# Sums of squares in three parts, two accumulators and two-slot rows in a two-layer hybrid kernel

## The chip, the cores and the metric

The kernel runs on one core of a Trainium2 chip. The metric is the device time of one execution in microseconds. PE is the matrix engine (TensorE), DVE is VectorE, ACT is ScalarE, POOL is GpSimd, and SP is the engine whose queue issues the DMAs.

## The reference

Two layers work on 640 tokens: 128 context tokens and 512 latent ones, of width 1024. The even layer's mixer is an mLSTM (4 heads) beside an HGRN2 (4 heads); the odd layer's is differential attention (8 heads). Each layer also has an FFN, and adaLN vectors (shift, scale, gate) that are computed from a conditioning vector. Cut to what the change touches:

```python
def _rmsnorm(x, g):
    xf = x.astype(f32)
    return xf * lax.rsqrt(jnp.mean(xf * xf, axis=-1, keepdims=True) + EPS) * g.astype(f32)

def _modulation(cond, w, b):
    mod = jnp.einsum('...d,de->...e', jax.nn.silu(cond.astype(f32)), w.astype(f32)) + b.astype(f32)
    return jnp.split(mod[..., None, :], 6, axis=-1)

# mLSTM, a chunk: the decay between two tokens weights the scores
dmat = jnp.where(tri, b[..., :, None] - b[..., None, :] + ic[..., None, :], -jnp.inf)
s = jnp.einsum('bhtd,bhsd->bhts', qc, kc) * jnp.exp(dmat - mt[..., None])

# a layer
hp = _rmsnorm(xp, norm_mix_g[l]) * (1.0 + sc_p) + sh_p    # and hs from xs alike, then the mixer
xp = xp + g_p * mp
hp = _rmsnorm(xp, norm_ffn_g[l]) * (1.0 + sc2_p) + sh2_p  # then the FFN
```

After the two layers a last RMSNorm gives the outputs.

## The kernel before

**Layout and order.** The residual `x` lies with features on partitions, as [128, 8, 640]: 8 blocks of 128 features, and the tokens as two halves of 320. A float32 product is three matmuls of high and low parts (`mm3`, whose matmuls all carry line 188). A scheduler orders each engine's instructions; in the mixer units and in the transitions PE keeps the order in which the program is written. The mixers run as eight units, four mLSTM heads and four HGRN2 heads. Between the steps of a unit, a `fill` object feeds PE with projection matmuls of coming units; it also holds a list of side jobs, which take their turn once so much matmul cost has been issued.

**The adaLN side units.** Most adaLN vectors are products on PE, but four units of four column blocks each run on ACT and GpSimd beside the mLSTM heads (`ada_vec`, L477 to L502). A unit loads 8 blocks of 256 KB of the weight (`araw`, two slots in the space of the tag `fb`, L483), multiplies each by the two conditioning vectors on ACT (16 products, L486, into `acc` or `atmp`), and adds them on GpSimd (14 adds of 128x512, L488). Then PE sums over partitions with four matmuls (`pj<-acc,ones`, L492), the result is copied, transposed and finished. There is one accumulator, in the space of the tag `qp`, and one unit is open at a time (the fourth argument of `add_side`, L1248). Ahead of the first HGRN2 unit (`u == H4`, L1249) all side jobs still open are carried out, and the HGRN2 work then takes over the tags `qp`, `fb`, `kc` and `kr`.

**The rows of the decay.** For each mLSTM head and each chunk of 128 tokens two rows of the decay are spread over all partitions by a DMA of 128 KB from DRAM on SP's queue (`rows_of`, L915). The tile `nb` has five slots in the space of the tag `kr`; the rows of head h + 1 are fetched chunk by chunk as VectorE's min with the causal mask (`weights`, L960) frees a slot, so the fetch is five chunks ahead. After the min come two exponentials on ACT (L964) and VectorE's product with the scores (L965).

**The norms.** `sq_sum` (L523) squares the 8 blocks of one half on ACT (L530). Blocks 1 to 5 are added to `sq` by GpSimd for half 0 and by VectorE for half 1 (L532); block 7 is added to block 6 in `s2` by VectorE (L534), which then joins the two (L535). `columns` (L592) takes the mean over the 1024 features for 64 tokens a matmul (5 for a half), adds epsilon on VectorE (`r`, L598), takes the power -1/2 on GpSimd (L599) and makes a diagonal on VectorE (`dg`, L601), which one more matmul spreads over the partitions (`spread`). Both run in three transitions: from the first mixer to its FFN, from there to the second layer's mixer, and from that to its FFN. The output norm (`to_output`, `chunk`) uses `sq_sum` too.

**The lambda vector.** The second transition also loads the four lambda rows of the odd layer (`lp`) and reduces them on VectorE (L1593 to L1598).

## Time and profile before

| | us |
|---|---|
| median of 3 runs | 1824.48 (1822.47 to 1824.6) |
| the profiled execution | 1827.93 |
| its span | 1826.1 |
| PE busy | 1739.6 (95%) |
| VectorE busy | 1379.0 (76%) |
| ScalarE busy | 805.2 (44%) |
| GpSimd busy | 493.5 (27%) |

The mean clock granted to PE is 0.983 of full speed. The span goes from the first to the last recorded instruction; the execution's own time is 1.8 us more. A line like `261.62 1.07 PE L188 MATMUL pj<-acc,ones ... [9.40 <-POOL acc L488]` says that PE's matmul into the bank `pj` starts at 261.62 us and takes 1.07 us, and that PE was idle for 9.40 us before it, until GpSimd's instruction of line 488 on `acc` ended.

### The profile page before, as it was taken

The page shows a single profiled execution, that of the slowest core. Times are in us where ns is not written, and L with a number is a line of the kernel's source. Part 1 is how long each engine was busy: PE and PEld are TensorE (multiplying, and loading weights), DVE is VectorE, ACT ScalarE, POOL GpSimd, SP SyncE. Part 2 cuts the span into 40 slices and gives each one's busy share as a digit, 9 for nine tenths or more (in the row PEclk, how much of TensorE's full clock was granted, in tenths as well). Part 3 has the DMA queues.
Part 4 walks back from the last instruction along what each step waited for, and adds up shares of the span by engine and source line. Part 5 has one row for each costly group of instructions (what it writes and reads, how often), then busy time and mean ns, then how long its engine had stood idle before and what let it go on. Part 6 is the DMA issues. An engine that isn't in the chain of part 4 may idle for free.

```text
span 1826.1 us, 31627 instructions
## 1 busy us (share of the span) xinstructions
PE 1739.6 (95%) x12198; PEld 1661.5 (91%) x12198; DVE 1379.0 (76%) x2806; ACT 805.2 (44%) x1677; POOL 493.5 (27%) x409
## 2 busy tenths in 40 slices
PE   7998979999889999999999899999989999999998
PEld 5798969999778999999998898999978999999998
DVE  5657766677797777777778687777879887888787
ACT  5466543343353333333324466566536332333334
POOL 2244443233122222223211221112121333232321
PEclk9999989999989999999999999999999999999999
DMA  9344222122615434443412221112031322222211
GB/s 310 116 133 133 82 79 58 53 75 66 208 50 162 125 120 137 137 141 116 128 58 81 67 86 44 31 54 76 24 121 58 93 79 84 82 81 76 87 59 59
DMA packets 187979, 174.80 MB, mean 96 GB/s; under 512 B 7762, under 2 KB 168372, under 8 KB 187828
## 3 DMA queue, kind: packets, MB, share of 16 engines
q1 hardware_dynamic: 186564, 172.63, 30.7%
q8 instruction: 97, 1.59, 0.4%
q14 instruction: 54, 0.44, 0.1%
q10 hardware_dynamic: 1264, 0.14, 0.1%
HBM read 167.99 MB, written 4.74 MB: 95 GB/s over the span
## 4 chain that ended last, share of the span: by engine, by line
PE 76%; DVE 12%; DMA 4%; ACT 4%; issue 3%; POOL 1%; SPq 1%; ACTq 0%; DVEq 0%; POOLq 0%
PE pj L188 59%; PE nm L188 8%; PE p L188 5%; PE s L188 2%; DMA araw<-in_ada_w_dram 2%; DVE wl L319 2%; PE p L193 1%; DVE x L371 1%; ACT wh L318 1%; ACT atmp L486 1%; DVE hl L570 1%; DMA raw<-in_ffn_w_dram 1%; DMA wg<-in_ev_w_in_dram 0%; DVE hh L564 0%; PE pj L193 0%
## 5 line engine op out<-in xcount | busy, mean ns | idle before, releaser
L188 PE MATMUL pj<-hh,wh 128*128 128x320 f32 x1648 | 526.6, 322 | 11.9 <-DVE hh L564 5.7
L188 PE MATMUL pj<-hh,wl 128*128 128x320 f32 x1648 | 513.7, 312 | 0.0
L188 PE MATMUL pj<-hl,wh 128*128 128x320 f32 x1648 | 502.6, 313 | 2.1 <-DVE hl L570 1.9
L188 PEld LDWEIGHTS pj<-hh,wh 128*128 128x128 f32 x1648 | 313.1, 190 | 27.0 <-DVE hh L564 9.4
L188 PEld LDWEIGHTS pj<-hl,wh 128*128 128x128 f32 x1648 | 310.5, 190 | 3.9 <-DVE hl L570 2.4
L188 PEld LDWEIGHTS pj<-hh,wl 128*128 128x128 f32 x1648 | 313.8, 190 | 0.0
L188 PE MATMUL pj<-t,wh 128*128 128x320 f32 x960 | 217.0, 311 | 0.2 <-ACT wh L1322 0.2
L318 ACT CAST wh<-raw 128x1024 fp32r<-128x1024 f32 x127 | 132.6, 1048 | 184.8 <-PE pj L188 88.1
L319 DVE TENSOR_TENSOR wl<-raw,wh 128x1024 fp32r<-128x1024 f32 x127 | 162.8, 1284 | 40.0 <-ACT wh L318 39.7
L188 PEld LDWEIGHTS pj<-t,wh 128*128 128x128 f32 x960 | 160.9, 188 | 3.4 <-DVE o L1374 0.8
L1322 ACT CAST wh<-s 128x1024 fp32r<-128x1024 f32 x80 | 84.1, 1051 | 151.7 <-PE pj L188 151.7
L188 PE MATMUL pj<-t,wl 128*128 128x320 f32 x480 | 148.9, 310 | 1.1 <-DVE wl L1323 1.1
L1336 POOL TENSOR_TENSOR s<-raw 128x512 f32<-128x512 f32 x40 | 55.9, 1397 | 333.1 <-DVE wl L1323 331.5
L371 DVE SCALAR_TENSOR_TENSOR x<-nm,g2h,x 128x128 f32<-128x128 f32 (+1 forms) x236 | 93.5, 429 | 48.7 <-PE nm L188 48.3
L188 PE MATMUL pj<-ah,wh 128*128 128x320 f32 x392 | 122.5, 313 | 0.0
L188 PE MATMUL pj<-al,wh 128*128 128x320 f32 x392 | 121.3, 310 | 0.0
L188 PE MATMUL pj<-ah,wl 128*128 128x320 f32 x392 | 121.2, 309 | 0.0
L371 DVE SCALAR_TENSOR_TENSOR x<-pj,g2h,x 128x128 f32<-128x128 f32 (+2 forms) x292 | 112.1, 430 | 12.0 <-PE pj L188 11.3
L1338 POOL TENSOR_TENSOR s<-s,raw 128x512 f32<-128x512 f32 x40 | 66.4, 1659 | 198.3 <-DVE wl L1323 198.3
L1323 DVE TENSOR_TENSOR wl<-s,wh 128x1024 fp32r<-128x1024 f32 x80 | 97.2, 1215 | 8.5 <-ACT wh L1322 8.4
L1322 ACT CAST wh<-raw 128x512 fp32r<-128x512 f32 (+1 forms) x81 | 67.9, 838 | 80.1 <-PE pj L188 80.0
L188 PE MATMUL nm<-al,wh 128*128 128x320 f32 x312 | 96.3, 311 | 1.6 <-DVE al L1438 1.6
(415 smaller groups left out, 3898.4 us busy)
## 6 DMA issues: line engine op xcount, KB each, us to landing
raw<-in_ffn_w_dram SPq DMA_DIRECT2D x132, 512.0 KB
own<-in_ada_w_dram SPq DMA_DIRECT2D x48, 512.0 KB
raw<-in_ev_w_in_dram SPq DMA_DIRECT2D x36, 512.0 KB
raw<-in_od_w_in_dram SPq DMA_DIRECT2D x24, 512.0 KB
raw<-in_ada_w_dram SPq DMA_DIRECT2D x20, 512.0 KB
araw<-in_ada_w_dram SPq DMA_DIRECT2D x32, 256.0 KB
araw<-in_ada_w_dram SPq DMA_DIRECT2D x12, 512.0 KB
raw<-in_ev_w_out_dram SPq DMA_DIRECT2D x8, 512.0 KB
```

The lines of the kernel that those rows point to most:

```text
L188: ins = nc.tensor.matmul(*args, **kw)
L193: ins = nc.tensor.transpose(*args, **kw)
L318: S.copy(wh, raw3)
L319: V.tensor_tensor(wl, raw3, wh.bitcast(F32), op=ALU.subtract)
L371: V.scalar_tensor_tensor(x[:, m, t0:t1], o[:, t0 - a * HALF:t1 - a * HALF], gate[:, m, c:c + 1], x[:, m, t0:t1], op0=ALU.mult, op1=ALU.add)
L486: S.activation(t, r, AF.Copy, scale=cpad[:, k, c:c + 1])
L570: order(V.tensor_tensor(hl[:, k, t], tmps[k], hh[:, k, t].bitcast(F32), op=ALU.subtract))
L1322: S.copy(wh, src)
L1323: V.tensor_tensor(wl, src, wh.bitcast(F32), op=ALU.subtract)
L1336: G.tensor_tensor(sa[:, 0], a21, a22, op=ALU.add)
L1338: G.tensor_tensor(sb[:, 0], sa[:, 0], a11, op=ALU.subtract)
```

## The change

Three parts, each of a few lines.

- **Two accumulators.** Two side units may be open at a time, and their accumulators alternate between the spaces of `kr` and `qp`. `araw` and `atmp` keep two slots each.
- **Rows in two slots.** The rows of the decay lie in two slots of the tile `sc`, in the order of all 20 (head, chunk) pairs, and each min fetches the rows two ahead. There are 20 fetches as before, 2 at the start and 18 within the heads.
- **Norms.** GpSimd adds the squares of blocks 1 to 5 in both halves. The squares of blocks 6 and 7 are not added: `sq_sum` returns the three partial sums, and each column of `columns` and `chunk` is three matmuls that accumulate in PSUM. 36 adds of 128x320 leave VectorE, 20 of them come to GpSimd, and PE has 72 more matmuls: in a transition 15 for a half in place of 5, in the output norm 18 in place of 6.

```diff
             if 0 < k < SQUARES:
-                (V if a else G).tensor_tensor(sq, sq, dst, op=ALU.add)
-            elif k > SQUARES:
-                V.tensor_tensor(s2, s2, dst, op=ALU.add)
-        V.tensor_tensor(sq, sq, s2, op=ALU.add)
-        return sq
+                G.tensor_tensor(sq, sq, dst, op=ALU.add)
+        return sq, s2, dst
...
             for i in range(NC64):
-                T.matmul(o[0:64, i:i + 1], lhsT=sq[:, i * 64:(i + 1) * 64], rhs=mean1, start=True, stop=True)
+                for j, part in enumerate(sq):
+                    T.matmul(o[0:64, i:i + 1], lhsT=part[:, i * 64:(i + 1) * 64], rhs=mean1, start=j == 0, stop=j == 2)
...
-    nb = ev.tile([P, NCH, 2, P], F32, tag="kr", name="nb", bufs=1)
-
-    def rows_of(h, c):
-
-        Q.dma_start(nb[:, c], nmd[h, c:c + 1].to_broadcast([P, 2, P]))
+    nb = tt("sc", 1)[:, 0:4 * P].rearrange("p (i r t) -> p i r t", i=2, r=2)
+
+    def rows_of(i):
+
+        h, c = divmod(i, NCH)
+        Q.dma_start(nb[:, i % 2], nmd[h, c:c + 1].to_broadcast([P, 2, P]))
...
-            V.tensor_tensor(dm, nb[:, c], caus, op=ALU.min)
-            if h + 1 < H4:
-                rows_of(h + 1, c)
+            i = h * NCH + c
+            V.tensor_tensor(dm, nb[:, i % 2], caus, op=ALU.min)
+            if i + 2 < H4 * NCH:
+                rows_of(i + 2)
...
+            accs = [0]
+
             def acc():
-                return ev.tile([P, 2, NT], F32, tag="qp", name="acc", bufs=1)[:, :, 0:512]
+                accs[0] += 1
+                a = ev.tile([P, 2, NT], F32, tag=("qp", "kr")[accs[0] % 2], name="acc", bufs=1)
+                return a[:, :, 0:512]
...
-            fill.add_side([ada_vec_gen(*i, raw, tmp, acc) for i in vec_units(VEC0)], VEC_EVERY, 1, eager=False)
+            fill.add_side([ada_vec_gen(*i, raw, tmp, acc) for i in vec_units(VEC0)], VEC_EVERY, 2, eager=False)
```

What stands where after the change, at three places. In the rows, xN counts equal instructions in a row, and the lines of the changed kernel are its own (L916 is the fetch of rows, L925 and L926 the state loads of a head, L946 the store of a state).

First, the queue of SP at the beginning of mLSTM head 3, whose state loads are the two into `cs`; `araw` are the loads of the side units, `raw` those of weights, `nb` or `sc` the rows of the decay. Before:

```order
L483 DMA araw<-in_ada_w_dram 128x512
L926 DMA cs<-in_state_mlstm_C_dram 128x128
L927 DMA cs<-in_state_mlstm_C_dram 128x128
L947 DMA out_mlstm_C_dram<-cf 128x2x128
L325 DMA raw<-in_ev_w_in_dram 128x8x128
L483 DMA araw<-in_ada_w_dram 128x512 x3
L325 DMA raw<-in_ev_w_in_dram 128x8x128
L483 DMA araw<-in_ada_w_dram 128x512 x2
L325 DMA raw<-in_ev_w_in_dram 128x8x128
L483 DMA araw<-in_ada_w_dram 128x512
L1138 DMA hst<-in_state_hgrn_S_dram 128x128
L483 DMA araw<-in_ada_w_dram 128x512
```

After:

```order
L483 DMA araw<-in_ada_w_dram 128x512
L916 DMA sc<-nmd 128x256
L483 DMA araw<-in_ada_w_dram 128x512 x3
L1061 DMA raw<-in_ev_w_in_dram 128x4x256
L916 DMA sc<-nmd 128x256
L483 DMA araw<-in_ada_w_dram 128x512
L916 DMA sc<-nmd 128x256
L925 DMA cs<-in_state_mlstm_C_dram 128x128
L926 DMA cs<-in_state_mlstm_C_dram 128x128
L916 DMA sc<-nmd 128x256
L946 DMA out_mlstm_C_dram<-cf 128x2x128
L325 DMA raw<-in_ev_w_in_dram 128x8x128
```

The seven loads of the fourth unit, which stood behind the state loads and the store `out_mlstm_C`, are no longer there; the last `araw` now stands ahead of the state loads, and fetches of rows stand where there were none.

At the same place of the program, GpSimd from the state copies of head 0 (the first two `cs`) on; `rst` is the power for a head's norm factors. Before:

```order
L928 COPY cs<-v_746 128x1
L929 COPY cs<-v_746 128x1
L488 TENSOR_TENSOR acc<-acc,atmp 128x512 x11
L948 COPY nout<-cf 128x2
L488 TENSOR_TENSOR acc<-acc,atmp 128x512 x3
L928 COPY cs<-v_746 128x1
L929 COPY cs<-v_746 128x1
L948 COPY nout<-cf 128x2
L689 TENSOR_TENSOR rst<-rst,mhalf 128x5
L488 TENSOR_TENSOR acc<-acc,atmp 128x512 x14
L928 COPY cs<-v_746 128x1
L929 COPY cs<-v_746 128x1
```

After:

```order
L927 COPY cs<-v_746 128x1
L928 COPY cs<-v_746 128x1
L488 TENSOR_TENSOR acc<-acc,atmp 128x512 x12
L947 COPY nout<-cf 128x2
L488 TENSOR_TENSOR acc<-acc,atmp 128x512 x13
L927 COPY cs<-v_746 128x1
L928 COPY cs<-v_746 128x1
L488 TENSOR_TENSOR acc<-acc,atmp 128x512 x2
L947 COPY nout<-cf 128x2
L488 TENSOR_TENSOR acc<-acc,atmp 128x512 x2
L687 TENSOR_TENSOR rst<-rst,mhalf 128x5
L488 TENSOR_TENSOR acc<-acc,atmp 128x512 x13
```

Before, the adds of one unit lie ahead of head 0's `rst`; now those of two units and one add of the third do.

Second, VectorE in the second transition, second half of the tokens; `r` and `dg` are the norm's factors and their diagonal, `l`, `ls` and `nl` belong to the lambda vector, `p` is a PSUM bank. Before:

```order
L570 TENSOR_TENSOR hl<-hf,hh 128x320
L534 TENSOR_TENSOR s_10876<-s_10876,s_10894 128x320
L570 TENSOR_TENSOR hl<-hf,hh 128x320
L535 TENSOR_TENSOR sq<-sq,s_10876 128x320
L598 TENSOR_SCALAR r<-p_10964 64x5
L1593 TENSOR_TENSOR l_11144<-lp 1x128
L1595 TENSOR_REDUCE ls<-l_11144 1x2
L601 TENSOR_TENSOR dg<-ident,r 64x320
L1598 SCALAR_TENSOR_TENSOR nl<-ls 1x1
```

After:

```order
L567 TENSOR_TENSOR hl<-hf,hh 128x320
L319 TENSOR_TENSOR wl<-raw,wh 128x1024
L567 TENSOR_TENSOR hl<-hf,hh 128x320
L1597 TENSOR_TENSOR l_11176<-lp 1x128
L1599 TENSOR_REDUCE ls<-l_11176 1x2
L1602 SCALAR_TENSOR_TENSOR nl<-ls 1x1
L596 TENSOR_SCALAR r<-p_10986 64x5
L599 TENSOR_TENSOR dg<-ident,r 64x320
```

The two joining adds of `sq` are gone, and the three ops of the lambda vector, which stood around the diagonal, are all ahead of `r`.

Third, GpSimd in the first transition, from the last add of the first half on; `r` is the power of the first half's factors, `s<-raw` are adds on weights of the FFN. Before:

```order
L532 TENSOR_TENSOR sq<-sq,s_5490 128x320
L1337 TENSOR_TENSOR s<-raw 128x512
L599 TENSOR_TENSOR r<-r,mhalf 64x5
L1336 TENSOR_TENSOR s<-raw 128x512
L1338 TENSOR_TENSOR s<-s,raw 128x512
L1339 TENSOR_TENSOR s<-raw,s 128x512
```

After:

```order
L532 TENSOR_TENSOR sq<-sq,s_5490 128x320
L532 TENSOR_TENSOR sq<-sq,s_5665 128x320
L1341 TENSOR_TENSOR s<-raw 128x512
L532 TENSOR_TENSOR sq<-sq,s_5668 128x320
L597 TENSOR_TENSOR r<-r,mhalf 64x5
L1340 TENSOR_TENSOR s<-raw 128x512
L532 TENSOR_TENSOR sq<-sq,s_5671 128x320
L1342 TENSOR_TENSOR s<-s,raw 128x512
L532 TENSOR_TENSOR sq<-sq,s_5674 128x320
L1343 TENSOR_TENSOR s<-raw,s 128x512
L532 TENSOR_TENSOR sq<-sq,s_5677 128x320
```

The five adds of the second half, which VectorE had, lie among these; two of them stand ahead of the power.

## Rows read from the trace of the kernel before

**Rows 1.** The page, parts 1 and 4: busy time of each engine (share of the span, instructions), and the chain that ended last by line.

```profile
PE 1739.6 (95%) x12198; PEld 1661.5 (91%) x12198; DVE 1379.0 (76%) x2806; ACT 805.2 (44%) x1677; POOL 493.5 (27%) x409
...
PE pj L188 59%; PE nm L188 8%; PE p L188 5%; PE s L188 2%; DMA araw<-in_ada_w_dram 2%; DVE wl L319 2%; PE p L193 1%; DVE x L371 1%; ACT wh L318 1%; ACT atmp L486 1%; DVE hl L570 1%; DMA raw<-in_ffn_w_dram 1%; DMA wg<-in_ev_w_in_dram 0%; DVE hh L564 0%; PE pj L193 0%
```

**Rows 2.** Busy time of each engine in five windows of 5 us at the end of mLSTM head 3: window, length, then busy us (instructions) of each engine, the clock granted to PE as a share of full speed, the DMA share and GB/s.

```profile
245.00:250.00 5.00, 2.36 (x17) 1.98 (x16) 3.94 (x7) 2.47 (x8) 2.48 (x2) 0.98 0.60 172
250.00:255.00 5.00, 2.22 (x9) 1.82 (x7) 3.13 (x9) 4.23 (x11) 2.50 (x2) 0.50 0.23 66
255.00:260.00 5.00, 0.00 (x0) 0.00 (x0) 3.17 (x6) 2.01 (x5) 3.87 (x4) 0.50 0.52 157
260.00:265.00 5.00, 3.23 (x13) 1.53 (x14) 3.29 (x3) 1.57 (x4) 4.18 (x4) 0.50 0.00 0
265.00:270.00 5.00, 5.00 (x37) 5.00 (x36) 2.18 (x4) 0.00 (x0) 1.17 (x1) 0.81 0.01 3
```

**Rows 3.** PE's timeline at the same place: start, us, instruction, and in brackets the idle time before it and what ended that.

```profile
249.17 0.27 PE L193 MATMUL p<-ident,nout 128*8 128x128 f32 x1 [2.64 <-issue]
...
251.75 0.47 PE L188 MATMUL pj<-hh,wl 128*128 128x320 f32 x1
261.62 1.07 PE L188 MATMUL pj<-acc,ones 128*32 128x256 f32 x4 [9.40 <-POOL acc L488]
```

**Rows 4.** The chain of waits followed back from 310 us: start, us, what. One row of mLSTM head 1 (the load of a row of the decay) and four of the fourth adaLN unit.

```profile
157.61 2.18 DMA nb<-nmd
...
222.80 4.12 DMA araw<-in_ada_w_dram
...
251.55 2.63 DMA araw<-in_ada_w_dram
254.26 1.34 ACT atmp L486 x2
255.62 3.29 DMA araw<-in_ada_w_dram
```

**Rows 5.** GpSimd's timeline, columns as in rows 3: where the adds of the second adaLN unit and of the fourth begin, and a later pair of the fourth.

```profile
134.66 5.55 POOL L488 TENSOR_TENSOR acc<-acc,atmp 128x512 f32<-128x512 f32 x4
...
231.96 2.54 POOL L488 TENSOR_TENSOR acc<-acc,atmp 128x512 f32<-128x512 f32 x2 [16.22 <-ACT atmp L486]
...
245.49 2.48 POOL L488 TENSOR_TENSOR acc<-acc,atmp 128x512 f32<-128x512 f32 x2 [1.18 <-ACT atmp L486]
```

**Rows 6.** VectorE's timeline at the end of head 3.

```profile
245.50 1.34 DVE L987 TENSOR_SCALAR hs<-inter,dn 128x128 f32<-128x128 f32 x1
...
250.23 0.29 DVE L987 TENSOR_SCALAR hs<-inter,dn 128x128 f32<-128x128 f32 x1
...
254.56 0.48 DVE L1049 SCALAR_TENSOR_TENSOR so<-so,pj 128x320 f32<-128x320 f32 x1
```

**Rows 7.** Windows as in rows 2: unit 0 runs in the first, none in the second, unit 1 in the third, unit 2 in the fourth.

```profile
88.00:112.00 24.00, 23.23 (x157) 22.65 (x156) 10.47 (x15) 17.01 (x30) 19.90 (x15) 1.00 0.56 166
112.00:134.00 22.00, 21.25 (x146) 19.75 (x146) 14.34 (x47) 13.84 (x45) 0.98 (x4) 1.00 0.41 121
134.00:166.00 32.00, 26.17 (x181) 25.12 (x180) 28.23 (x52) 21.62 (x49) 20.87 (x17) 1.00 0.47 141
185.00:208.00 23.00, 22.47 (x154) 21.91 (x153) 19.58 (x44) 15.08 (x35) 18.46 (x14) 1.00 0.38 115
```

**Rows 8.** VectorE's timeline in head 1: the mins that use rows of the decay.

```profile
120.95 0.43 DVE L960 TENSOR_TENSOR dm<-nb,caus 128x256 f32<-128x256 f32 x1
...
127.34 0.42 DVE L960 TENSOR_TENSOR dm<-nb,caus 128x256 f32<-128x256 f32 x1 [0.24 <-PE p L188]
```

**Rows 9.** Waits of SP's queue between 60 and 270 us: line, waited for, us in total, times, the longest.

```profile
SPq L483 <- ACT atmp L486: 17.0, 11, 4.2
```

**Rows 10.** The sums of squares by their tile: operation and count, then ns (least, median, most), first and last start; the last two rows tell who waited for them (us, times).

```profile
L532 POOL TENSOR_TENSOR sq<-sq,s x20: 867/877/882, 491.4 to 1806.1; 128x320 f32<-128x320 f32 x20
L532 DVE TENSOR_TENSOR sq<-sq,s x20: 473/480/2623, 500.6 to 1812.5; 128x320 f32<-128x320 f32 x20
...
L188 PE MATMUL pj<-mean,sq x10: 189/197/198, 500.4 to 500.9; 128*64 128x1 f32 x10
...
L535 DVE TENSOR_TENSOR sq<-sq,s x8: 472/481/1452, 499.7 to 1816.5; 128x320 f32<-128x320 f32 x8
...
  PE p L188: 2.7, 1
  PE pj L188: 1.4, 1
```

**Rows 11.** PE's timeline in the first transition: the column sums of one half.

```profile
500.35 0.71 PE L188 MATMUL pj<-mean,sq 128*64 128x1 f32 x10 [1.42 <-DVE sq L535]
```

**Rows 12.** VectorE's timeline in the second transition (second half of the tokens) and in the third.

```profile
1011.41 0.28 DVE L1593 TENSOR_TENSOR l<-lp 1x128 f32<-1x128 f32 x1 [4.23 <-DMA lp<-in_od_lambda_dram]
...
1011.93 0.47 DVE L601 TENSOR_TENSOR dg<-ident,r 64x320 f32<-64x320 f32 x1
...
1361.32 2.62 DVE L532 TENSOR_TENSOR sq<-sq,s 128x320 f32<-128x320 f32 x1 [0.32 <-ACT s L530]
```

**Rows 13.** GpSimd's timeline in the third transition.

```profile
1361.18 1.17 POOL L599 TENSOR_TENSOR r<-r,mhalf 64x5 f32<-64x5 f32 x1
```

**Rows 14.** The diagonal of the norm's factors by its tile: who waited for it (us, times).

```profile
  PE p L188: 3.5, 2
```

More of the change, by code (lines that the diff above doesn't have):

```diff
@@ L1012, in ml_mix @@
         mix["last"] = last
-    for c in range(NCH):
-        rows_of(0, c)
+    for i in range(2):
+        rows_of(i)
     def hg_bounds():
@@ L1847, in chunk @@
                     if t0 < t1:
-                        T.matmul(o[t0 - c * P:t1 - c * P, 0:1], lhsT=sqs[a][:, t0 - a * HALF:t1 - a * HALF],
-                                 rhs=mean1, start=True, stop=True)
+                        for j, part in enumerate(sqs[a]):
+                            T.matmul(o[t0 - c * P:t1 - c * P, 0:1], lhsT=part[:, t0 - a * HALF:t1 - a * HALF],
+                                     rhs=mean1, start=j == 0, stop=j == 2)
                 V.tensor_scalar(rcol[:, c:c + 1], o[:, 0:1], EPS, None, op0=ALU.add)
```

## The prediction

> **What bounds the kernel now.** I read the page first, then the busy time in short stretches, then the timelines of PE, GpSimd and VectorE where PE is idle. PE is busy for 95% of the span and its projection matmuls alone are 59% of the chain that ended last [rows 1]. So time comes back only where PE stands idle or runs at a low clock, and every matmul added beside busy PE work costs its full time.
>
> The one large hole is at 245 to 270 us, at the end of the last mLSTM head. In five windows of 5 us PE is busy 2.36, 2.22, 0.00, 3.23 and 5.00 us [rows 2], an idle sum of 2.64 + 2.78 + 5.00 + 1.77 = 12.2 us. Behind the idle the granted clock reads 0.50 (the level of 1.2 GHz) in three windows and 0.81, between the two levels, in the last, against 0.98 ahead of it. Work at 0.50 takes twice its time, so 2.22 x 0.5 + 3.23 x 0.5 + 5.00 x 0.19 = 3.7 us more are lost. The hole costs 15.9 us.
>
> What ends it is the fourth adaLN unit: PE's `pj<-acc,ones` waits 9.40 us for GpSimd's add at L488 [rows 3]. The chain of waits says why it is late [rows 4]: its first load is issued at 222.80, and then load (2.63 to 4.12 us) and two ScalarE products (1.34 us) follow each other in series, up to the last load at 255.62. The load couldn't start earlier: all units share one accumulator (`qp`), which the third unit's matmul on PE gives back only then, though GpSimd is idle ahead of 231.96 for 16.22 us [rows 5].
>
> **Part 1: two accumulators.** By the order of SP's queue, the fourth unit's loads, which stood behind the state loads of head 3 (L926, L927), now stand ahead of them; on GpSimd no add stands behind head 3's copies. The stretches thus shift by one unit: unit 1, which ran from 134.66 on [rows 5], runs directly behind unit 0, unit 2 in the stretch of unit 1, unit 3 in that of unit 2.
> The gain: the 15.9 us of the hole. The 2.64 us ahead of 249.17 are counted as gone too, since VectorE ops there run slow beside the adds: L987 takes 1.34 us at 245.50, beside GpSimd's adds at 245.49, and 0.29 us at 250.23 [rows 5, 6].
> What is late next: the projection behind the hole needs a bank that VectorE empties (`so`, L1049) at 254.56 + 0.48 = 255.04 [rows 6], 2.8 us after PE fell idle at 252.2. With the slow ops in front of it gone it comes earlier; bounds 0 and 2.8, I take 1.0, nearer to the lower end because a good 2 us of slow ops precede it.
> The cost: unit 1 now runs at about 112 to 135 us, where none ran. With a unit running, PE loses 24 - 23.23 = 0.8, 32 - 26.17 = 5.8 and 23 - 22.47 = 0.5 us in the three stretches; in 112 to 134, without one, 0.75 [rows 7]. The mean of the three is 2.4; head 0's power of the norm factors now stands on GpSimd behind all of unit 1's adds, and I add 1.1, less than one 1.27 us add. Taken 3.5, bounds 0 and 7 (the worst stretch and one add).
> Sum: -15.9 + 1.0 + 3.5 = -11.4, bounds -15.9 and -6.1.
>
> **Part 2: rows in two slots.** The first accumulator's partner takes the space of the rows' five slots, so rows are loaded two ahead. A row's slot comes free with V's min (L960), and the next but one min wants it: the shortest such spacing is 120.95 to 127.34, 6.4 us [rows 8]. The load needs 2.18 us [rows 4] and about 0.4 us of issue, so alone it is in time. Ahead of it on SP's queue may stand an adaLN load that waits for ScalarE: 11 such waits, 17.0 us, the longest 4.2 [rows 9]. 2.18 + 0.4 + 4.2 = 6.8 passes the shortest spacing by 0.4. Behind a late row wait the exponentials and the head's products. Taken +0.5, bounds 0 and 3.
>
> **Part 3: the norms.** Off VectorE go 20 adds of the second half and 16 joining adds, each 0.48 us, 17 us in all; onto GpSimd come 20 adds of 0.88 us, 17.5 us [rows 10]. Neither engine bounds the span. On the path stand these:
> PE's column sums, 3 matmuls in place of 1. The first call took 0.71 us for 10 records of about 0.197 us [rows 10, 11], so a step of (0.71 - 0.197) / 9 = 0.057 us; 20 more records are 1.14 us, six calls 6.8 us. In the output norm the extra ones stand in a tail with idle PE, and I add 0.5: +7.3.
> Where PE waits for the sum (2.7 and 1.4 us, [rows 10]), two adds of 0.48 leave the chain: -0.95 in three transitions and once in the output, -3.8.
> In the third transition VectorE's add took 2.62 us beside GpSimd's power at 1361.18 [rows 12, 13]. That add leaves VectorE, and the factors' diagonal behind it gets ahead by 2.62 - 0.48 = 2.1. It is what PE waits for, 3.5 us in two places [rows 14]: -2.1.
> In the first transition two more adds of 0.88 us stand ahead of the power on GpSimd, of which none or both may fall into idle time: between 0 and 1.8, taken +0.9.
> In the second, VectorE's order puts the first op on the lambda vector (`l<-lp`, L1593) ahead of the factors `r` and the diagonal, and it waited for its load until 1011.41 [rows 12]. Before, only the diagonal (1011.93) stood behind it, while the power of 1.17 us ran beside the wait. Now `r`, the power and the diagonal come after the load: about +2.2, less up to 1 because the load's own wait starts earlier: +1.7.
> Sum: 7.3 - 3.8 - 2.1 + 0.9 + 1.7 = +4.0. VectorE's 17 us of relief gives something back where its work ends a wait of PE, which the rows don't price singly; I take -1 for it and so +3.0. Bounds: if all waits of these rows vanish (-2.7 - 1.4 - 3.5) and half the calls' matmuls hide in them (+3.4), -4.2; if nothing comes back, 7.3 + 1.8 + 2.2 = +11.3.
>
> **A rule that speaks against it.** The row at 245.50 shows a VectorE op held for 1.05 us beside GpSimd adds of 1.24 each [rows 5, 6], and 1361.32 one held for 2.1 us [rows 12]. The Trainium skill, "SBUF — State Buffer", section "SBUF: two separate sides", calls the port pair that the two engines share an exclusive lock: of a GpSimd op and a VectorE op in a two-port mode or with two SBUF inputs, the one that starts first has the pair for its whole instruction, and the other stands still. The trace agrees (0.29 against 1.34 us). By it in full, the 34 adds that change their place would hold up VectorE for their 35.3 us, and the sum would be +23.9; by the rows of the stretches with a unit it is the 3.5 above.
>
> **The rivals.**
> 1. More comes back. Unit 1 is covered like the first and third (0.8 in place of 3.5), nothing is late behind the hole (0 in place of 1.0), the norms end at -3: -15.9 + 0.8 + 0.5 - 3.0 = -17.6, a median of 1806.9. For it: PE lost only 0.8 and 0.5 us in two stretches of three. Against: PE pays for each added matmul beside busy work.
> 2. The gain is mostly eaten. Unit 1 costs 5.8 as at 134 to 166, the emptied bank is late by 2.8, the norms cost +6: -15.9 + 5.8 + 2.8 + 0.5 + 6.0 = -0.8, 1823.7. For it: 134 to 166 is the same kind of stretch (head 0 ends, head 1 begins).
> 3. Slower, through GpSimd and VectorE holding each other up. 14 adds of unit 1 (1.27 us each, 17.8) and 20 of the norms (17.5) now lie in stretches where VectorE feeds PE, 35.3 us in all. If a VectorE op on PE's path stands still for half of each, that is 17.7 us in place of unit 1's 3.5: -15.9 + 1.0 + 17.7 + 0.5 + 3.0 = +6.3, 1830.8. It decides from a third of each add on (11.4 / 35.3 = 0.32). Against: the stretches at 88 and 185 us hold as many adds (19.90 and 18.46 us of GpSimd) and PE lost 0.8 and 0.5 us [rows 7].
> 4. The second accumulator does nothing, because the raw rows have two slots only: 0 + 0.5 + 3.0 = +3.5, 1828.0. The order on SP and GpSimd speaks against it: the fourth unit's work is ahead of head 3's there.
>
> **How the numbers follow.** Sum: -11.4 + 0.5 + 3.0 = -7.9, taken -7.5 in round numbers, against the profiled execution's 1827.93 us: 1820.4. That execution is 3.45 us above the median of the runs shown, so I take the difference off the median: 1824.5 - 7.5 = 1817.0 us. 0.2% is 3.65 us, about what a measurement of this kernel can tell from no change.
> Chances: forecast 0.58, rival 1 0.14, rival 2 0.19, rival 3 0.07, rival 4 0.02. Faster by over 0.2% (below 1820.8): forecast and rival 1, 0.72. Within: rivals 2 and 4, 0.21. Slower: 0.07. The range of 1807 to 1824 leaves out rivals 3 and 4 (0.09) and about a third of rivals 1 and 2 (0.10).
>
> **What would show it.** In the profile after: `pj<-acc,ones` no longer waits at about 260 us and PE is busy from 253 on with a clock of 0.9 or more; GpSimd's last add at L488 ends by about 210. PE loses 2 to 6 us more than before in 112 to 135. Each column call lasts about 1.9 us, the waits for the sum are under 2 us together, and `l<-lp` stands ahead of `r` with the diagonal 1 to 2 us late. Wrong would be: a hole of PE that moved to another place near 250, VectorE ops of over 1 us all through 112 to 135, or a wait for the row at L960.

## The result, and the profile after

| | median, us | runs | range, us |
|---|---|---|---|
| before | 1824.1 | 6 | 1822.47 to 1825.78 |
| after | 1837.72 | 6 | 1834.12 to 1843.4 |

The changed kernel is slower: the ratio is 1.0066, with a 95% interval of 1.0049 to 1.0082. The profiled execution took 1838.81 us (span 1837.0, mean clock 0.981), 10.9 us more than the one of before.

Where the time went is read by setting the same instruction of both traces side by side (start in each timeline, us):

| landmark | before | after | later by |
|---|---|---|---|
| mLSTM head 0 scaled by its norm (VectorE, `hs<-hs,rst`) | 137.44 | 145.82 | 8.4 |
| head 1 scaled | 173.85 | 185.87 | 12.0 |
| head 2 scaled | 215.63 | 227.61 | 12.0 |
| first square of the first transition | 488.93 | 488.91 | 0.0 |
| first square of the second transition | 976.59 | 978.66 | 2.1 |
| last head of the second mixer scaled (GpSimd, `oh<-oh,rst`) | 1341.31 | 1348.14 | 6.8 |
| first square of the output norm | 1800.53 | 1808.81 | 8.3 |
| end of the span | 1826.1 | 1837.0 | 10.9 |

So the two accumulators win nothing in all: 12.0 us are lost by the end of head 2 and given back at the hole. The norms lose 2.1 us by the second transition, 4.7 by the end of the second mixer, 1.5 by the output norm and 2.6 in it.

These are two single executions, and single executions differ by several us. Seven traces have the first mixer of before (before, e1, e4 to e7 and e11 of the experiments below); they reach the first square of the first transition between 486.48 and 491.38. Head 2 is scaled at 215.59 to 216.70 in them, and at 224.59 to 227.61 in the three with both accumulators (after, e2, e12): 8 to 12 us later. From there to the scaling of head 4 they take 104.42 to 106.82 us, the three 92.88 to 94.48: 10 to 14 us come back at the hole. Two of the norms' losses are clear of this spread. From the first square of the second transition to that of the third, after and e1 take 376.99 and 376.13 us, the other fifteen traces 368.60 to 372.99. From the first square of the output norm to the end, the six traces with sums in three parts take 28.0 to 28.5 us, the other eleven 25.3 to 26.3.

The page of after, part 1, and then windows of 10 us (columns as in [rows 2]):

```profile
PE 1754.1 (95%) x12342; PEld 1677.4 (91%) x12342; DVE 1359.4 (74%) x2770; ACT 805.3 (44%) x1677; POOL 511.0 (28%) x429
```

```profile
110.00:120.00 10.00, 8.83 (x60) 8.50 (x59) 6.49 (x21) 6.59 (x16) 7.06 (x6) 1.00 0.58 177
120.00:130.00 10.00, 8.07 (x56) 7.56 (x56) 8.83 (x12) 7.03 (x19) 7.22 (x6) 1.00 0.56 145
130.00:140.00 10.00, 8.27 (x50) 7.38 (x49) 6.69 (x16) 7.18 (x22) 4.93 (x7) 0.83 0.39 118
140.00:150.00 10.00, 4.53 (x27) 4.27 (x26) 5.63 (x14) 5.13 (x10) 7.31 (x6) 0.83 0.42 117
150.00:160.00 10.00, 7.70 (x42) 7.36 (x41) 9.68 (x16) 6.46 (x14) 8.52 (x7) 0.83 0.40 120
250.00:260.00 10.00, 10.00 (x71) 9.79 (x70) 5.12 (x15) 4.10 (x14) 0.00 (x0) 1.00 0.22 59
260.00:270.00 10.00, 8.12 (x57) 7.32 (x56) 5.20 (x12) 2.05 (x5) 1.17 (x1) 0.83 0.23 61
```

The hole of [rows 2] is gone: PE is busy 10.00 of 10 us from 250 on. But a smaller wait stands behind it, for the bank that VectorE empties (`so`), and the clock of that window reads 0.83:

```profile
264.51 0.39 PE L188 MATMUL pj<-wh,hh 128*128 128x256 f32 x1 [1.88 <-DVE so L1049]
```

In place of the hole PE stands idle at 110 to 160 us, 5.47 us in the window at 140 alone, and from 130 on the granted clock is 0.83, between the two levels, where [rows 7] shows 1.00.

What PE waits for there (PE's timeline of after):

```profile
129.76 0.66 PE L193 MATMUL p<-ident,k 128*128 128x128 f32 x4 [1.93 <-ACT inter L979]
132.15 0.33 PE L193 MATMUL p<-ident,k 128*128 128x128 f32 x1 [1.73 <-DVE inter L981]
...
147.75 1.33 PE L193 MATMUL p<-ident,hs 128*128 128x128 f32 x5 [5.47 <-DVE hs L866]
...
160.67 1.20 PE L188 MATMUL p<-cs,q 128*128 128x258 f32 x2 [2.97 <-DVE cs L951]
```

The four waits make 1.93 + 1.73 + 5.47 + 2.97 = 12.1 us. The last two stand in the trace of before as well, shorter:

```profile
139.14 0.76 PE L193 MATMUL p<-ident,hs 128*128 128x128 f32 x5 [2.61 <-DVE hs L868]
...
149.01 0.67 PE L188 MATMUL p<-cs,q 128*128 128x258 f32 x2 [2.49 <-DVE cs L952]
```

So the waits grew by 12.1 - 5.1 = 7.0 us. The lower clock is most of the rest: PE is busy for 8.27 + 4.53 + 7.70 = 20.5 us in the three windows at 0.83, and 17% of that is an estimated 3.5 us.

The longest wait is for head 0's scaling. GpSimd's timeline of after shows what that waited for last:

```profile
136.58 1.29 POOL L488 TENSOR_TENSOR acc<-acc,atmp 128x512 f32<-128x512 f32 x1 [1.07 <-ACT atmp L486]
...
143.38 1.26 POOL L488 TENSOR_TENSOR acc<-acc,atmp 128x512 f32<-128x512 f32 x1 [2.69 <-ACT atmp L486]
144.61 1.18 POOL L687 TENSOR_TENSOR rst<-rst,mhalf 128x5 f32<-128x5 f32 x1
145.76 5.79 POOL L488 TENSOR_TENSOR acc<-acc,atmp 128x512 f32<-128x512 f32 x4
```

and VectorE's:

```profile
142.71 0.16 DVE L686 TENSOR_SCALAR rst<-ss 128x5 f32<-128x5 f32 x1
145.82 1.88 DVE L866 TENSOR_TENSOR hs<-hs,rst 128x640 f32<-128x640 f32 x1 [2.94 <-POOL rst L687]
...
156.41 2.27 DVE L938 TENSOR_SCALAR vw<-vv,cols 128x129 f32<-128x129 f32 x2
```

VectorE had head 0's mean squares ready at 142.71 + 0.16. GpSimd's power `rst` on them started at 144.61 only: ahead of it in the queue stood the first add of unit 2, and that add waited 2.69 us for ScalarE's product. That costs 1.7 us. The larger part came earlier, since before had its mean squares 9.4 us sooner:

```profile
133.26 0.17 DVE L688 TENSOR_SCALAR rst<-ss 128x5 f32<-128x5 f32 x1 [0.67 <-ACT junk L990]
```

In after VectorE's ops on that way are slow beside unit 1's adds: from 121 to 131 us six small ones take 1.05 to 1.50 us each, where before at 112 to 134 us has none above 1 us but the weights' `wl`. (The scaling itself is only 9.4 + 1.7 - 2.7 = 8.4 us later, since in before two `vw` ops of 2.30 us stood between the power and it.) The scaling `hs` took 1.88 us beside the next adds, 1.64 in before. The two `vw` ops at 156.41, which are the wait for `cs` ahead of 160.67, took 2.27 us together, and 2.29 in before.

In the second transition the lambda vector's op holds up the whole norm (VectorE's timeline of after, the counterpart of [rows 12]):

```profile
1014.75 0.28 DVE L1597 TENSOR_TENSOR l<-lp 1x128 f32<-1x128 f32 x1 [5.11 <-DMA lp<-in_od_lambda_dram]
...
1015.69 0.14 DVE L596 TENSOR_SCALAR r<-p 64x5 f32<-64x5 f32 x1
1017.12 0.48 DVE L599 TENSOR_TENSOR dg<-ident,r 64x320 f32<-64x320 f32 x1 [1.29 <-POOL r L597]
```

PE's matmul on the diagonal, before and then after:

```profile
1012.45 0.80 PE L188 MATMUL p<-dg,ones 64*128 64x320 f32 x2 [1.96 <-DVE dg L601]
```

```profile
1017.66 1.43 PE L188 MATMUL p<-dg,ones 64*128 64x320 f32 x2 [4.71 <-DVE dg L599]
```

`r` and the power, which ran ahead of the wait before, now follow it, and PE's wait for the diagonal grew from 1.96 to 4.71 us. PE then works at 1.2 GHz (granted clock 0.50):

```profile
1012.00:1018.00 6.00, 1.29 (x8) 1.03 (x7) 1.26 (x5) 0.20 (x1) 1.18 (x1) 0.91 0.50 173
1018.00:1022.00 4.00, 4.00 (x13) 3.14 (x13) 1.79 (x5) 1.99 (x6) 0.00 (x0) 0.50 0.00 0
```

At the end of the kernel PE's last transposes of one chunk (`nm<-ident,xg` x8) start at 1830.76 and take 1.95 us, at 1.2 GHz (1.09 us in before):

```profile
1822.00:1826.00 4.00, 3.59 (x33) 3.15 (x31) 1.93 (x4) 3.40 (x8) 2.60 (x4) 1.00 0.31 123
1826.00:1830.00 4.00, 3.23 (x26) 2.90 (x25) 1.67 (x4) 0.81 (x3) 1.10 (x2) 0.91 0.47 189
1830.00:1834.00 4.00, 2.71 (x13) 2.31 (x12) 0.96 (x3) 1.30 (x2) 0.55 (x1) 0.50 0.50 204
```

PE had idled in part of the stretch ahead, the clock fell to 0.50, and the last outputs come later by that.

A column call is as long as was worked out (PE's timeline of after, first and last row of the first call): it lasts from 498.83 to 500.74, 1.91 us.

```profile
498.83 0.28 PE L188 MATMUL pj<-mean,sq 128*64 128x1 f32 x2
...
500.37 0.37 PE L188 MATMUL pj<-mean,s 128*64 128x1 f32 x4
```

### The profile page after: what moved, and what is told of

Its sections match the earlier page's. It is cut to its first block, busy times and chain, and to the rows that moved or that the text cites. A ratio compares the mean times of both kernels' runs of the same rounds, so it can differ in the third digit from the quotient of the medians.

```text
span 1837.0 us, 31894 instructions
## 1 busy us (share of the span) xinstructions
PE 1754.1 (95%) x12342; PEld 1677.4 (91%) x12342; DVE 1359.4 (74%) x2770; ACT 805.3 (44%) x1677; POOL 511.0 (28%) x429
```

## The experiments

Each group was timed together with the kernel before on one chip. The first group (e1 to e4) had 1825.07 us as its median of before (21 runs), e5 to e8 1822.44 (25 runs), e9 to e12 1825.16 (31 runs), e13 to e15 1825.76 (18 runs). "Against before" is the difference of the medians in each group. The ratio with its 95% interval is estimated apart from it, and for e1 and e4 it gives 2.6 us more than the medians do; the intervals are some 2 to 4 us to either side.

**e1: the norms alone.**

```diff
-                (V if a else G).tensor_tensor(sq, sq, dst, op=ALU.add)
+                G.tensor_tensor(sq, sq, dst, op=ALU.add)
...
-        return sq
+        return sq, s2, dst
```

with the matmuls of three parts in `columns` and `chunk`; rows and accumulators as before.

> The kernel before with the third part alone (three partial sums to PE, all adds of squares on GpSimd). Theory: the norms account for the whole loss (by the traces +2.1 us in the first transition, +4.7 in the second, +1.5 in the third, +2.6 in the output norm), so +10.9 us, about 1835. Rival: the norms cost about +3 us as predicted and the rest comes from the other two parts, so about 1827.

Measured 1838.76 us (4 runs), +13.7 against before, ratio 1.0089 (1.0068 to 1.0109). The norms are the whole loss. The trace (of the slowest of the four runs) has a row that explains part of it, in the first transition (VectorE's timeline of e1, then GpSimd's, then PE's):

```profile
506.17 5.62 DVE L599 TENSOR_TENSOR dg<-ident,r 64x320 f32<-64x320 f32 x1 [0.57 <-POOL r L597]
```

```profile
504.97 1.17 POOL L597 TENSOR_TENSOR r<-r,mhalf 64x5 f32<-64x5 f32 x1
506.12 1.26 POOL L1334 TENSOR_TENSOR s<-raw 128x512 f32<-128x512 f32 x1
507.33 0.85 POOL L532 TENSOR_TENSOR sq<-sq,s 128x320 f32<-128x320 f32 x1
508.15 1.26 POOL L1336 TENSOR_TENSOR s<-s,raw 128x512 f32<-128x512 f32 x1
509.37 0.85 POOL L532 TENSOR_TENSOR sq<-sq,s 128x320 f32<-128x320 f32 x1
510.19 1.26 POOL L1337 TENSOR_TENSOR s<-raw,s 128x512 f32<-128x512 f32 x1
```

```profile
511.94 1.40 PE L188 MATMUL pj<-dg,ones 64*128 64x320 f32 x2 [5.91 <-DVE g2h L472]
```

The diagonal took 5.62 us; in the trace of after the same op starts at 504.39 and takes 0.48 us. It became ready as GpSimd's power ended, and GpSimd's next op started at 506.12. VectorE's op did not end until GpSimd's row of five ops, one directly behind the other, ended at 511.45, and PE waited 5.91 us. In the trace of after GpSimd's next op after the power waited there for a load until 505.13, so the diagonal ran before it.

**e2: two accumulators and two-slot rows, norms as before.** The edit is the other hunks of the change:

```diff
+                a = ev.tile([P, 2, NT], F32, tag=("qp", "kr")[accs[0] % 2], name="acc", bufs=1)
...
-VEC_EVERY, 1, eager=False)
+VEC_EVERY, 2, eager=False)
```

> The kernel before with two accumulators and two-slot rows, norms as before. Theory: the 16 us of the hole at 245 to 270 us are won and about as much is lost at 100 to 190 us, where unit 1 now runs beside the end of head 0: 1824, within 3 us either way. Rival (the norms cost only 3): these two parts hold the loss, about 1832.

Measured 1823.24 us (10 runs), -1.8 against before, ratio 0.9989 (0.9975 to 1.0003): the theory's number. In its trace head 2 is scaled 9.0 us later than in before's (224.59) and head 4 4.8 us earlier (317.47): 13.7 us come back at the hole.

**e3: the second accumulator for the fourth unit alone.**

```diff
-                a = ev.tile([P, 2, NT], F32, tag=("qp", "kr")[accs[0] % 2], name="acc", bufs=1)
+                a = ev.tile([P, 2, NT], F32, tag="kr" if accs[0] == 4 else "qp", name="acc", bufs=1)
```

on e2.

> As the run with two accumulators and two-slot rows, but only the fourth unit gets the second accumulator: units 0, 1 and 2 share the first, so on GpSimd unit 1's adds stay behind head 0's power, and the fourth unit's adds begin right behind the third's. Theory (the loss at 100 to 190 us is unit 1's move): the hole goes and nothing is paid there, 12 to 16 us faster than before, 1808 to 1812. Rival (the loss comes from rows that are fetched only two ahead): it stays, 1822 to 1826.

Measured 1818.07 us (10 runs), -7.0, ratio 0.997 (0.9959 to 0.9982). Half of what the theory asked. Head 0 and head 1 are scaled within 1.4 us of before (137.27 and 175.20), so unit 1's move is what delayed them, and rows fetched two ahead do not; but the fourth unit's adds now delay head 2 (221.62, 6.0 us later than before).

**e4: the norms with the lambda vector behind the diagonal.**

```diff
-            V.tensor_tensor(dg, ident[0:64, 0:64].unsqueeze(1).to_broadcast([64, NC64, 64]),
+            ff["dgi"] = V.tensor_tensor(dg, ident[0:64, 0:64].unsqueeze(1).to_broadcast([64, NC64, 64]),
...
-    V.tensor_tensor(l2, lp2[:, :, 0], lp2[:, :, 1], op=ALU.mult)
+    with tc.issue_after(ff["dgi"].ins):
+        V.tensor_tensor(l2, lp2[:, :, 0], lp2[:, :, 1], op=ALU.mult)
```

on e1.

> As the run with the norms alone, but VectorE's first op on the lambda vector may only start behind the second transition's last diagonal, so its wait for the load holds up nothing of the norm. Theory (of the +4.7 us in the second transition some 3 come from that order): 2.5 to 4 us less than the norms alone. Rival (PE's wait for the diagonal is set by the three-part sums, not by the lambda load): no change against the norms alone.

Measured 1831.57 us (6 runs), +6.5, ratio 1.005 (1.003 to 1.007): 7.2 us less than e1, twice the expectation. The intervals of the two touch, but the traces put the difference where the op stands: from the first square of the second transition to that of the third e1 takes 376.13 us and e4 368.60. In VectorE's timeline of e4 the diagonal no longer waits for the load:

```profile
1006.88 0.48 DVE L599 TENSOR_TENSOR dg<-ident,r 64x320 f32<-64x320 f32 x1 [1.29 <-POOL r L597]
1009.04 0.28 DVE L1592 TENSOR_TENSOR l<-lp 1x128 f32<-1x128 f32 x1 [1.68 <-DMA lp<-in_od_lambda_dram]
```

**e5: the same order in the kernel before.** The edit of e4 on before.

> The kernel before with one change: VectorE's first op on the lambda vector may only start behind the second transition's last diagonal (as in the run of the norms with that order). In the trace of before the diagonal stood at 1011.93, the power of GpSimd that it needs was done at about 1008.4. Theory: the order costs the kernel before some 3 us too, so 3 to 4 us faster than before, 1820 to 1821. Rival: the lambda wait hurts only the changed norms, no change.

Measured 1821.95 us (10 runs), -0.5, ratio 0.9994 (0.998 to 1.0007). The rival holds: before, that order cost nothing that can be measured, though its diagonal waited too.

**e6: three partial sums only.** On e5, the second half's adds stay on VectorE:

```diff
+                (V if a else G).tensor_tensor(sq, sq, dst, op=ALU.add)
+        return sq, s2, dst
```

> Lambda behind the diagonal, and of the norms' change only the three partial sums: PE takes three matmuls a column, the two joining adds are gone, the second half's five adds stay on VectorE. Theory (the loss comes from GpSimd's adds that hold VectorE up): little is lost against the run with the lambda order alone, 0 to 4 us. Rival (PE's 72 more matmuls are the loss): 8 to 10 us slower than that run.

Measured 1824.35 us (10 runs), +2.4 against e5, ratio to before 1.0005 (0.9991 to 1.0019): within the theory's 0 to 4, and by the intervals not clear of 0. The trace has it in the output norm, which takes 28.01 us to the end, 26.19 in e5.

**e7: moved adds only.** On e5, the joining adds and single matmuls as before:

```diff
-                (V if a else G).tensor_tensor(sq, sq, dst, op=ALU.add)
+                G.tensor_tensor(sq, sq, dst, op=ALU.add)
```

> Lambda behind the diagonal, and of the norms' change only the move: the second half's 20 adds go to GpSimd, the joining adds and the single matmul a column stay as before. Theory (GpSimd's adds hold VectorE up): 5 to 10 us slower than the run with the lambda order alone. Rival (the added matmuls are the loss): within 2 us of it.

Measured 1826.67 us (10 runs), +4.7 against e5, ratio to before 1.0018 (1.0008 to 1.0028). A little under the theory's 5 to 10, well over the rival's 2. Together 2.4 + 4.7 = 7.1, and e4, which has both, stands at +6.5 where e5 stands at -0.5, which is 7.0. By the medians the two add up, more closely than the intervals allow to claim.

The first transition shows how the moved adds cost time. VectorE's timeline of e7, then GpSimd's, then PE's:

```profile
503.58 4.04 DVE L473 TENSOR_SCALAR g2h<-g2h 128x4 f32<-128x4 f32 x1
```

```profile
503.48 0.86 POOL L532 TENSOR_TENSOR sq<-sq,s 128x320 f32<-128x320 f32 x1
...
506.33 1.26 POOL L1339 TENSOR_TENSOR s<-raw,s 128x512 f32<-128x512 f32 x1
```

```profile
508.16 1.40 PE L188 MATMUL pj<-dg,ones 64*128 64x320 f32 x2 [4.72 <-DVE dg L601]
```

A VectorE op on 128x4 elements, which takes 0.15 us in before (508.46), stands still until GpSimd's row of adds without a pause ends at 507.59. The diagonal is next in VectorE's queue, and PE waits 4.72 us for it, 1.50 in e5. From this transition's first square to the next one's e7 takes 490.93 us and e5 485.17. A late sum is not the reason: PE's longest wait for it is 1.65 us in e7, 4.24 in e5.

**e8: short adds in the side units.** On e2:

```diff
-                    G.tensor_tensor(a[:, c], a[:, c], t, op=ALU.add)
+                    G.tensor_tensor(a[:, c, 0:64], a[:, c, 0:64], t[:, 0:64], op=ALU.add)
```

> Two accumulators and two-slot rows with the norms as before, and GpSimd's adds of the side units on 64 of the 512 columns only: it leaves out the sum of the other columns, so the adaLN vectors of these units are not computed. Loads and ScalarE's products stay as they are, GpSimd's part of a unit falls from 18 us to some 4. Theory (what eats the hole's 16 us is GpSimd's adds, through the queue ahead of head 0's power and through VectorE held up): 10 to 13 us faster than the same kernel with whole adds, 1810 to 1813. Rival (the loads and ScalarE's products of unit 1 delay the heads): no change against it, 1821 to 1825.

Measured 1805.84 us (4 runs), -16.6, ratio 0.99 (0.9877 to 0.9924). With the adds short 14.8 us more are won than in e2. Not all of them are unit 1's move: the edit shortens the adds of all four units, and head 2 is scaled not only 12.9 us earlier than in e2 but 4.0 us earlier than in before (211.68). From there to head 4 14.1 us come back. No run has short adds in the order of before, so what the adds cost there already is known only from this difference. The windows from 88 us to the scaling of head 1, of before, of e2 and of e8:

```profile
88.00:173.85 85.85, 77.24 (x521) 73.60 (x520) 56.44 (x122) 56.67 (x137) 43.13 (x37) 1.00 0.48 144
```

```profile
88.00:182.87 94.87, 81.61 (x522) 77.58 (x521) 64.50 (x123) 65.53 (x151) 61.80 (x51) 0.95 0.50 151
```

```profile
88.00:169.32 81.32, 77.73 (x515) 73.93 (x514) 43.35 (x123) 65.48 (x153) 19.48 (x51) 0.98 0.58 177
```

The same 123 VectorE instructions are busy for 64.50 us beside whole adds and for 43.35 us beside short ones: by this difference 21 us of VectorE's "busy" time is standing still. In before it is 13 us, with 56.44 us for 122 instructions; the two accumulators add 8. ScalarE's wait for a free product slot, 4.2 us in before, is gone as well; it was, in e2 (waits in that stretch: us, times, longest):

```profile
ACT atmp L486 <- POOL acc L488: 8.3, 10, 1.8
```

**e9: the side units' sums on VectorE.** On e2:

```diff
-                S.activation(t, r, AF.Copy, scale=cpad[:, k, c:c + 1])
-                if k:
-                    G.tensor_tensor(a[:, c], a[:, c], t, op=ALU.add)
+                if k:
+                    V.scalar_tensor_tensor(a[:, c], r, cpad[:, k, c:c + 1], a[:, c], op0=ALU.mult, op1=ALU.add)
+                else:
+                    S.activation(a[:, c], r, AF.Copy, scale=cpad[:, k, c:c + 1])
```

> Two accumulators and two-slot rows, norms as before, and the side units' sums taken off GpSimd and ScalarE: VectorE multiplies a raw block and adds it to the accumulator in one op (56 ops of 128x512, by the 0.55 us of a 128x320 op of that kind an estimate of 0.8 us each, 45 us of VectorE in all); ScalarE keeps the first product of each. Theory (unit 1's cost is GpSimd's adds, that hold VectorE up and stand ahead of head 0's power): 1812 to 1820, though VectorE has more work. Rival (any work beside head 0 and head 1 costs as much, since VectorE is what is short there): 1823 or more.

Measured 1822.86 us (10 runs), -2.3, ratio 0.9986 (0.9977 to 0.9995). Near the rival's number. Taken off GpSimd, the sums cost VectorE 0.75 us each (56 ops, 40.2 us), and head 0 is scaled as late as with GpSimd's adds (144.56). But the number does not speak of the heads alone: the first square of the first transition comes 1.8 us earlier than in e2 (483.67 against 485.44), and that of the second 3.8 us later. Between them stands a wait of PE for `hf` that e2's trace does not have; e10 has it too.

**e10: the same in the order of e3.** The edits of e3 and e9 together.

> The same sums on VectorE in the order of the kernel in which only the fourth unit has the second accumulator. Theory: GpSimd's adds cost there too (that kernel won 7 us of the hole's 16), so 3 to 8 us faster than it, 1810 to 1815. Rival: VectorE becomes the bound of the heads, 1820 or more.

Measured 1825.41 us (10 runs), +0.3, ratio 1.0001 (0.999 to 1.0012), against -7.0 for e3. That is the rival's number, but not for its reason. The first mixer ends only 1.5 us later than in e3 (first square at 485.89 against 484.38). 5.1 us more are lost from there to the second transition's first square, where no sum of a side unit runs any more; in the first transition PE waits, in e10 (and in e9 at 512.38, as long):

```profile
514.92 0.63 PE L188 MATMUL pj<-hh,wh 128*128 128x320 f32 x1 [6.97 <-DVE hf L548]
```

In e3 PE waits there 0.80 and 1.20 us, for `hh`. Why e9 and e10 wait for `hf` in its place stays open. So e9 and e10 don't decide whether VectorE is a worse place for the sums than GpSimd.

**e11: the norms with short moved adds.** On e4:

```diff
-                G.tensor_tensor(sq, sq, dst, op=ALU.add)
+                w = slice(0, 40 if a else HALF)
+                G.tensor_tensor(sq[:, w], sq[:, w], dst[:, w], op=ALU.add)
```

> The norms' change with lambda behind the diagonal (+6.5 us), but the second half's adds on GpSimd take 40 of the 320 columns: it leaves out most of the sum of squares of the second half, so the norm's factors of these tokens are not the right ones. The adds stand where they stood in the order and last some 0.2 us in place of 0.88. Theory (their length holds up VectorE and the power): 3 to 5 us less than with whole adds, 1825 to 1828. Rival (their place in the queue or the matmuls are the cost): as with whole adds, 1830 to 1833.

Measured 1825.32 us (10 runs), +0.2, ratio 1.0 (0.9988 to 1.0012), 6.3 us less than e4's +6.5. These 6.3 us, though measured on two chips, go with the adds' length, not with their place in the queue, which is the same. The matmuls of three parts, which stay, cost no more than the interval's 2 us here, net of the 36 adds that VectorE is rid of.

**e12: the whole change with the lambda vector behind the diagonal.** The edit of e4 on the changed kernel.

> The changed kernel whole, with only the lambda vector's first op behind the second transition's last diagonal. Theory (the order of that op costs the changed norms about 7 us, as between the two runs of the norms alone): 7 us faster than the changed kernel, 1829 to 1832. Rival (the difference of those two runs came from elsewhere in the order): 1835 to 1839.

Measured 1830.64 us (10 runs), +5.5, ratio 1.0031 (1.0021 to 1.0041): 8.1 us less than the changed kernel's +13.6 against its own before.

**e13 and e14: no power in the head norms.** On before (e13) and on e2 (e14):

```diff
-        G.tensor_tensor(r, r, mhalf[:, 0:NCH], op=ALU.pow)
         return r
```

> The kernel before without GpSimd's power -1/2 in the head norms: it leaves out the power, so the heads of the even layer are scaled by the mean square in place of its inverse root. It is the base for the next run. The eight powers take 1.2 us each, and each head's end waits for one: 0 to 8 us faster than before, on either theory.

> Two accumulators and two-slot rows, norms as before, and the same power of the head norms left out, so that no head's end waits for GpSimd's queue, while the adds of the side units stay whole and hold VectorE as they did. Theory of the queue (unit 1's adds ahead of head 0's power are what eats the hole's gain): 8 to 14 us faster than the run of the kernel before without the power. Theory of the port (VectorE held up by the adds is what eats it): within 4 us of that run, as the same two kernels with the power (1.8 us).

Measured 1824.34 us (10 runs), -1.4, for e13 and 1818.08 us (7 runs), -7.7, for e14 (ratios 0.9994, 0.9981 to 1.0007, and 0.995, 0.9934 to 0.9966). e14 is 6.3 us below e13, between the two theories: with the power the same step was worth 1.8, so by the medians the queue ahead of the power accounts for some 4.5 us of the 14.8 that e8 gives back. With intervals of 2.4 to 2.9 us for each of the three runs it may be anything from 0 to 9. The traces show little of a queue. Without the power head 0 is still scaled 10.6 us later in e14 (143.36) than in e13 (132.77). And in e2 the power, at 141.85, waits for VectorE's mean squares, whose op on 128x5 takes 1.24 us in place of 0.16:

```profile
140.53 1.24 DVE L688 TENSOR_SCALAR rst<-ss 128x5 f32<-128x5 f32 x1
```

**e15: the second accumulator for the third unit alone.** As e3 with `accs[0] == 3`.

> As the kernel in which one unit alone has the second accumulator, but the third in place of the fourth: GpSimd has 5 of its adds ahead of head 1's power, and all adds of the fourth ahead of head 3's. Theory of the queue: the 5 adds delay head 1 as unit 1 delayed head 0, 1818 to 1823, no better than the kernel with the fourth unit alone (1818.1). Theory of the port: the adds are spread over heads 1 and 2 and the last of them no longer collide with head 3, 1812 to 1817.

Measured 1817.04 us (6 runs), -8.7, ratio 0.9965 (0.9948 to 0.9983): at the upper end of the port's numbers, below the queue's. Its head 1 is scaled 7.0 us later than before (180.88), and head 3 0.4 us earlier (259.19). The delay of head 1 is one that the theory of the queue had forecast too, but its trace has no queue there. GpSimd's power waits for VectorE, and behind it VectorE's own ops stand between the power and the scaling:

```profile
174.68 1.19 POOL L689 TENSOR_TENSOR rst<-rst,mhalf 128x5 f32<-128x5 f32 x1 [0.93 <-DVE rst L688]
```

```profile
177.50 2.32 DVE L940 TENSOR_SCALAR vw<-vv,cols 128x129 f32<-128x129 f32 x2
```

Two `vw` ops take 0.48 us in before (at 175.19).

## Why the prediction was wrong

1817.0 us were predicted, in 1807 to 1824, with 0.72 for faster; it came out at 1837.72. By its steps:

- **The hole's cause was right, its price too high.** One shared accumulator was the cause, and the fourth unit is early enough with two, so rival 4 is out. But -15.9 + 1.0 = -14.9 was counted, and 12.1 us come back between head 2 and head 4 in the trace of after, 13.7 in e2, 12.1 in e12. The term for what is late next was too small: the wait for the bank that VectorE empties is 1.88 us, in place of 1.0, and PE works through that window at a clock of 0.83.
- **The cost of unit 1 failed.** "Taken 3.5, bounds 0 and 7" was read from PE's lost time in the stretches with a unit [rows 7]. It measured 12.0 us in the trace of after, 9.0 in e2 and 9.9 in e12. The rows were of stretches in which one unit ran beside one head; after, units 0, 1 and 2 run one behind the other through the end of head 0, the beginning of head 1 and head 2's projections. The sign that was named for being wrong is there: VectorE ops of over 1 us at 121 to 131. What costs the time is the length of the adds (e8), and the traces show by which way: VectorE held up, 8 us more than in before up to head 1's scaling. ScalarE's wait for product slots that GpSimd frees doubles, from 4.2 to 8.3 us. The queue ahead of the power, for which 1.1 us were added, is 1.7 us in the trace of after, where the add ahead of it waited 2.69 us for a load and a product, and nothing in e2's; by e13 and e14 it is 4.5, not clear of 0. How much of the cost is VectorE and how much ScalarE was not separated: e9 takes both away, but loads VectorE with 40.2 us of new work and loses time elsewhere.
- **The norms' sum failed, by two of its terms.** +3.0 was taken (bounds -4.2 and +11.3); e1 measured +13.7. The 72 matmuls and the joining adds together were about right: 7.3 - 3.8 = +3.5 predicted, +2.4 in e6. The lambda vector's order was counted at +1.7; it costs 7.2 (e1 against e4) to 8.1 us (e12). The wait itself was right in kind, `r`, power and diagonal behind the load, but the load came no earlier, and PE, idle for 4.7 us, then worked at half its clock. The moved adds were counted only where they stood ahead of a power (+0.9), with a gain of 2.1 for a VectorE add that no longer gets held up and 1 us for the relief of VectorE, -2.2 in all. e7 measured +4.7, e11 shows that it is their length, and the traces of e7 and e1 show VectorE held up ahead of a diagonal for which PE waits. The gain of 2.1 did not come: in the third transition another VectorE op is held up (`g2h`, 1.71 us at 1371.45), and PE's wait for the diagonal grew from 1.51 us in before to 2.63. Of the gains for the sum two came, the waits of 1.4 and 2.7 us in the first and second transition. In the third no wait stands ahead of the column call before (1360.06), and in the output norm the second half's sum was ready 16.5 us behind the first square in both traces.
- **A row at hand was read as one op too few.** The prediction put the 2.62 us at 1361.32 [rows 12] down to GpSimd's power [rows 13], which ends at 1362.35. VectorE's add ends only at 1363.94, behind GpSimd's next op, which ends at 1363.59 (trace of before):

```profile
1362.33 1.26 POOL L1339 TENSOR_TENSOR s<-raw,s 128x512 f32<-128x512 f32 x1
```

- **The rows were right.** VectorE waited for a row's load twice, 1.0 us in all, against 0.5 taken.
- **Rival 3 named the mechanism** (0.07), VectorE held up by the added GpSimd work, and priced it at 17.7 us for half of each moved add. What measured is 9 to 12 for unit 1 and 4.7 for the norms, 14 to 17. What it had against it, the covered stretches at 88 and 185 us, was taken as proof that a head hides such adds. VectorE is held up at 185 us of before too (ops of 1.06 to 1.27 us at 191.92, 193.03 and 201.06); PE loses 0.5 us there. That it has projections of earlier heads queued there is a likely reason and was not tested. That the rival's 1830.8 came out near e12's 1830.64 is luck in part, since it also counted the hole too high; the lambda order makes the remaining 7.

**On the rule of the Trainium skill** (SBUF — State Buffer, "SBUF: two separate sides"): the trace of e1 agrees that the loser stands still for a whole instruction of the other, and goes further, since VectorE's op at 506.17 stood still for five instructions of GpSimd in a row. The sum of +23.9 that the prediction worked out by the rule in full was too high: +13.6 measured, the lambda order's 7 to 8 included.

## What to carry to other kernels

An add that is moved from VectorE to GpSimd was not off VectorE here: where it runs beside VectorE's work, its length has to be counted as a possible wait of VectorE too, and a queue of such ops without a pause as one long one (5.62 us in e1, 4.04 in e7). Buffers that let a background job start earlier also move it beside other work, so the price has to be read where it will run, with what stands behind it in each queue. An op that waits for a load belongs behind the ops that something else waits for: the lambda vector's place in VectorE's queue cost 7 to 8 us of the changed kernel, and nothing measurable before the change. The part of this change that pays is a second accumulator for one late unit only: 8.7 us (e15) and 7.0 us (e3) less than before, where the change is 13.6 us more. The two are not apart by their intervals.

## What the runs showed of the hardware

- VectorE's op can be held up through several GpSimd ops that follow each other without a pause: 5.62 us for a diagonal that takes 0.48 us (e1), 4.04 us for an op on 128x4 that takes 0.15 (e7). In e1 GpSimd's next op had started 0.05 us ahead of the diagonal (506.12 against 506.17). In the trace of after it started 0.74 us behind it (505.13 against 504.39), and the diagonal took 0.48 us. Such near meetings may be why the changed kernel's runs spread over 9.3 us, against 3.3 of before in the same comparison. It isn't shown: before spreads over 7 to 11 us in the groups of the experiments.
- The profile counts a VectorE op that stands still as busy: 64.50 us and 43.35 us for the same 123 instructions (e2, e8). A busy share doesn't tell work from waiting there; the least duration of the same form does.
